# The keys' weights on ScalarE in place of GpSimd, and the bonus selector in one instruction

## The chip, the cores and the metric

The kernel runs on one core of a Trainium2 chip. The metric is the device time in microseconds (us) of one execution. An execution has five engines that work side by side, each strictly in the order of its own queue: TensorE (PE: matmuls; its weight loads are PEld), VectorE (DVE), ScalarE (ACT), GpSimd (POOL) and SyncE (SP), which here issues the loads of the weights.

## The reference, cut to what matters

Two layers over 256 tokens of width 1024, in float32. Layer 0 is an RWKV-7 time mix and a SwiGLU feed-forward block, layer 1 a rotary block attention and another feed-forward block. The change is in the time mix of layer 0:

```python
xr, xw, xk, xv, xa, xg = [x + xx * mu[n] for n in range(6)]
r, k, v = jnp.einsum('nbtc,ncd->nbtd', jnp.stack([xr, xk, xv]), w_rkv)
a = jax.nn.sigmoid(a0 + (xa @ a1) @ a2)
g = jax.nn.sigmoid(xg @ g1) @ g2
kk = heads(k * k_k)
kk = kk / jnp.maximum(jnp.sqrt(jnp.sum(kk * kk, -1, keepdims=True)), 1e-12)
k = k * (1 + (a - 1) * k_a)          # the keys' weights
...                                  # decays, the recurrence over time: y
bonus = jnp.sum(rh * kh * r_k, -1, keepdims=True) * vh
y = (y + bonus.reshape(B, T, C)).astype(x.dtype)
return (y * g) @ w_o
```

The weight of a key is a * k_a + (1 - k_a): one multiplication and one addition, with k_a and 1 - k_a constant along the tokens. The sum in the bonus is a matmul with a selector of heads that carries r_k.

## The kernel before

Channels lie on the 128 partitions, tokens along the free dimension, so a vector over channels is a column of `vec`, and an operation on 128 channels and 256 tokens is a 128x256 instruction.

**Weights.** Each weight matrix arrives in pieces of 512 KB over SP's queue into three raw buffers (`Stream.run`). ACT casts a piece to `hi`, a rounded copy, and DVE (or POOL for pieces listed in `PL`) computes `lo = raw - hi`. PE multiplies hi and lo separately, so a product of 128x512 is three matmuls. A raw buffer is free again when `lo` is done.

**Order of work.** The kernel is a set of generators (`weigh`, `keys`, `inverse`, `merge`, `recurrence`, the dense products `v_part` and so on) that yield what they wait for. A planner (`Issue.run`) holds a cost model of the engines (`Clock`), asks each generator when it could go on, and takes the ready one of the lowest rank. What it issues becomes each engine's fixed order. So a change of one instruction's engine or cost also changes the order in which later instructions stand on every engine. `yield I.idle("DVE")` makes a part wait until the modelled DVE is free. A generator added with the flag `True` (thin) is passed over where the model sees TensorE's clock low.

**The time mix.** `decays`, `gate` and `norms` give E (the decays), a and the raw kk (`kkr`) on ACT; `weigh(u)`, for u = 0 to 3, makes the weights `ka` of two slices of 128 channels in one half-slot and multiplies k by them on DVE, then makes `KB` and `a<-a,E`, which read the exponentials E. `on("ka")` is POOL since "ka" stands in the list `OFF`. `start()` makes `selrk`, the selector of the bonus. Later `scores` give the matrices SC of each chunk of 64 tokens, and `inverse` inverts their 32x32 diagonal blocks by 31 steps of two DVE operations on `TT`; DVE then transposes the result into `TN` and back into `SC` (STREAM_TRANSPOSE), and `merge` joins the blocks on PE: the products `n` (from TN) and then `t` (from SC and TN). After t the recurrence over the chunks (z, u, s, y) begins. The matmuls `v` (256 tokens by 1024 values) and `g` have no part in that chain; PE does them where the planner sees it free. Every engine instruction is recorded at the helper's line L300, so groups below go by tiles:

```python
yield ev(f"TN{hp}")
for q, hs in parts:
    for i in range(16):
        mm(nps[q][hi, i * 32:(i + 1) * 32], blk(hp, 0, 1)[:, q * 16 + i, :], TN[lo, q * 16 + i, :], True, True)
    I.after(nps[q][hi], lambda q, hs: act.copy(out=TN[hi, hs, :], ...), q, hs)
yield from fill(FILLI[hp])
yield ev(f"back1{hp}")
```

In this `merge`, `fill` lets a few v matmuls in before t.

Of the kernel before, what the change touches and what calls it, by code (L numbers as in the profile page):

```python
# [10 lines left out]
AF = mybir.ActivationFunctionType  # L11
ALU = mybir.AluOpType
# [7 lines left out]
KT = D // 128  # L20
# [39 lines left out]
NARROW = (slice(0, 512), slice(512, 768), slice(768, 1024))  # L60
LAST = ((WIDE, WIDE), (WIDE, NARROW))
OUTS = (1, 1)
OFF = ('ka', 'kk1', 'xxv')
MIXR = 'dve'
MIXA = "dve"
BON = 'pool'
# [28 lines left out]
MU, W0, A0, KK, KA, RK, GNG, GNB = 0, 48, 56, 64, 72, 80, 88, 96  # L95
# [327 lines left out]
def trunk(ctx, tc, a, out):  # L423
    nc = tc.nc
    clk = Clock()
    act, dve, pool = Engine(tc, nc.scalar, "ACT", clk), Engine(tc, nc.vector, "DVE", clk), Engine(tc, nc.gpsimd, "POOL", clk)
# [20 lines left out]
    def slot(shape, name, dtype=F32):  # L447
        return tp.tile([128] + shape, dtype, tag="t4", name=nm(name))
# [4 lines left out]
    def half_slot(name, dtype=F32):  # L453
        return sm.tile([128, 2, T], dtype, tag="w2", name=nm(name), bufs=6)

    I = Issue(clk)
    E = {}

    def ev(name):
        return E.setdefault(name, Event())  # L460
# [9 lines left out]
    def mm(ps, lhsT, rhs, start, stop, **kw):  # L470
        pe.matmul(ps, lhsT, rhs, start=start, stop=stop, **kw)
# [15 lines left out]
    vec = const.tile([128, 104], F32, name="vec")  # L487
# [5 lines left out]
    for u in range(4):  # L493
        q, o = u // 2, (u % 2) * 2
# [10 lines left out]
    sel2 = cst[:, 512:514]  # L505
# [3 lines left out]
    omka = const.tile([128, 8], F32, name="omka")  # L509
    dve.tensor_scalar(omka, vec[:, KA:KA + 8], -1.0, 1.0, ALU.mult, ALU.add)  # L510
    selrk = const.tile([128, KT, 2], F32, name="selrk")
# [28 lines left out]
    def c4(x):  # L540
        return x.rearrange("p a (c t) -> p a c t", c=NC)

    def on(name):
        return pool if name in OFF else dve

# [95 lines left out]
    def shifts():  # L641
        for u in range(4):
            q, o = u // 2, (u % 2) * 2
            yield xT[q][:, o:o + 2, :]
            pool.tensor_tensor(xx[q][:, o:o + 2, :], xT[q][:, o:o + 2, 0:T], xT[q][:, o:o + 2, 1:T + 1], ALU.subtract)
# [46 lines left out]
    av, Ev = [slot([4, T], "a") for _ in range(2)], [slot([4, T], "E") for _ in range(2)]  # L692
# [80 lines left out]
    def norms(u):  # L773
# [5 lines left out]
        sq = half_slot("sq")  # L779
        if "sq" in OFF:  # L780
            pool.tensor_tensor(sq, kkr[g][:, o:o + 2, :], kkr[g][:, o:o + 2, :], ALU.mult)
# [31 lines left out]
    def weigh(u):  # L813

        g, o = u // 2, (u % 2) * 2
        yield ev(f"k{u}")
        yield ev(f"a{g}")
        yield I.idle("DVE")
        w = half_slot("ka")
        for j in range(2):  # L820
            p = u * 2 + j
            on("ka").tensor_scalar(w[:, j, :], av[g][:, o + j, :], vec[:, KA + p:KA + p + 1], omka[:, p:p + 1],
                              ALU.mult, ALU.add)
        for j, x in enumerate(ksrc[u]):
            js = slice(0, 2) if len(ksrc[u]) == 1 else j
            dve.tensor_tensor(kg[g][:, o:o + 2, :][:, js], x, w[:, js], ALU.mult)
        I.reach(ev(f"ka{u}"), kg[g][:, o:o + 2, :])
        yield ev(f"G{g}")
        yield I.idle("DVE")
        for hp in range(2):  # L830
            r = HALF[hp]
            on(f"kb{hp}").tensor_tensor(KB[u][r, :, :, hp, :], c4(kg[g][r, o:o + 2, :]), c4(Gi[g][r, o:o + 2, :]), ALU.mult)
        yield I.idle("DVE")
        on("av").tensor_tensor(av[g][:, o:o + 2, :], av[g][:, o:o + 2, :], Gi[g][:, o:o + 2, :], ALU.mult)
        I.reach(ev(f"kd{u}"), KB[u], av[g][:, o:o + 2, :])
# [825 lines left out]
    def start():  # L1661
        mix(0, "xk", 2, early_slot, True)
        yield from shifts()
        I.reach(ev("xx"), *xx)
        mix(2, "xr", 0, early_slot, eng=dict(pool=pool, dve=dve)[MIXR])
        yield ev("xr")
        for p in range(KT):
            pool.tensor_scalar(selrk[:, p, :], sel2, vec[:, RK + p:RK + p + 1], None, ALU.mult)

    I.add(0, start())  # L1670
    I.add(0, W.run())
    I.add(1, lora())
    for g in range(2):
        I.add(1, decays(g))
    for u in range(4):
        I.add(2, norms(u), True)
        I.add(3, weigh(u))
# [97 lines left out]
```

## Time and profile before

| what | value |
|---|---|
| median of three runs | 750.04 us (747.36 to 753.28) |
| the profiled execution: time, span | 746.08 us, 744.3 us |
| mean granted clock of TensorE in it | 0.959 of full |
| busy: PE / PEld / DVE / ACT / POOL | 689.4 / 587.6 / 539.7 / 382.2 / 185.0 us |
| share of the span | 93% / 79% / 73% / 51% / 25% |

The busy shares are means over a program with stages of different limits, and idle time of an engine that nobody waits for costs nothing. A matmul's record ends late by its pipeline, so the pace of a row of matmuls is read from start to start. The granted clock stands in tenths or as a fraction of full speed: 1.00 is 2.4 GHz and 0.50 is 1.2 GHz.

### The profile page before, as it was taken

What the parts mean: (1) busy time and instruction counts of PE and PEld (TensorE: products, weight loads), DVE (VectorE), ACT (ScalarE), POOL (GpSimd) and SP (SyncE); (2) the same over time, 40 slices, a digit from 0 to 9 for tenths busy, and PEclk for the clock granted to TensorE, in tenths of its full rate; (3) what the DMA queues carried; (4) which work ended last, traced back from release to release, by engine and by line L of the source; (5) the groups of instructions that cost most, each with busy time, mean ns of one, the idle gap of its engine ahead of it and who ended that gap; (6) DMA issues with size and microseconds to landing.
All of it is one profiled execution on the core that took longest, in us unless ns stands there. A gap on an engine that the chain in (4) does not pass through costs nothing.

```text
span 744.3 us, 11759 instructions
## 1 busy us (share of the span) xinstructions
PE 689.4 (93%) x4500; PEld 587.6 (79%) x4500; DVE 539.7 (73%) x915; ACT 382.2 (51%) x679; POOL 185.0 (25%) x132
## 2 busy tenths in 40 slices
PE   6899795998889999999999699999979999999995
PEld 5799684777678888888888488777769888888885
DVE  7989999948897766656657935977776665666576
ACT  5974134456545554554556324756635545545550
POOL 5777964343463000000001613113040000000000
PEclk9999898779899999999999889999989999999999
DMA  6445312120565655655557615345046556555551
GB/s 242 152 147 187 107 57 86 57 83 7 188 223 172 227 178 190 196 183 187 197 182 240 201 34 182 125 142 199 28 170 195 178 194 197 175 194 192 187 160 56
DMA packets 33576, 117.21 MB, mean 157 GB/s; under 512 B 3808, under 2 KB 4832, under 8 KB 33520
## 3 DMA queue, kind: packets, MB, share of 16 engines
q1 hardware_dynamic: 31936, 110.89, 44.6%
q10 hardware_dynamic: 1584, 5.57, 2.5%
q8 instruction: 35, 0.57, 0.3%
q14 instruction: 21, 0.17, 0.1%
HBM read 115.40 MB, written 1.05 MB: 156 GB/s over the span
## 4 chain that ended last, share of the span: by engine, by line
PE 68%; DVE 8%; ACT 2%; DMA 2%; issue 1%; DVEq 0%; ACTq 0%
PE gu L300 29%; PE acc L300 14%; PE qkv L300 9%; PE o L300 5%; DVE xtok L300 3%; PE gn L300 2%; PE v L300 1%; PE tr L300 1%; DMA raw<-in_w_qkv_dram 1%; DVE sc L300 1%; PE ptr L300 1%; PE pv L300 1%; PE n L300 1%; ACT hi L300 1%; PE att L300 1%
## 5 line engine op out<-in xcount | busy, mean ns | idle before, releaser
L300 DVE TENSOR_TENSOR lo<-raw,hi 128x1024 fp32r<-128x1024 f32 (+1 forms) x172 | 210.3, 1228 | 144.6 <-ACT hi L300 144.4
L300 ACT CAST hi<-raw 128x1024 fp32r<-128x1024 f32 (+1 forms) x214 | 212.0, 999 | 186.2 <-issue 93.1
L300 PE MATMUL gu<-xw,hi 128*128 128x512 f32 x640 | 226.1, 395 | 0.0
L300 PE MATMUL gu<-xw,lo 128*128 128x256 f32 x640 | 179.8, 281 | 0.0
L300 POOL TENSOR_TENSOR lo<-raw,hi 128x1024 fp32r<-128x1024 f32 (+1 forms) x41 | 87.8, 2158 | 261.3 <-ACT hi L300 257.6
L300 PEld LDWEIGHTS gu<-xw,hi 128*128 128x128 f32 x640 | 120.3, 188 | 27.1
L300 PEld LDWEIGHTS gu<-xw,lo 128*128 128x128 f32 x640 | 120.9, 189 | 0.7
L300 PE MATMUL acc<-hi,hl 128*128 128x512 f32 (+1 forms) x180 | 53.8, 369 | 0.0
L300 PE MATMUL acc<-lo,hh 128*128 128x512 f32 (+1 forms) x180 | 53.7, 368 | 0.0
L300 PE MATMUL acc<-hi,hh 128*128 128x512 f32 (+1 forms) x180 | 53.5, 366 | 0.0
L300 PE MATMUL qkv<-hi,xhi 128*128 128x512 f32 x96 | 40.7, 424 | 2.3 <-ACT xhi L300 2.3
L300 PE MATMUL qkv<-hi,xlo 128*128 128x512 f32 x96 | 39.3, 409 | 0.0
L300 ACT ACTIVATE silu<-silu 128x256 f32<-128x256 f32 x40 | 16.7, 417 | 44.0 <-DVE silu L300 44.0
L300 PE MATMUL qkv<-lo,xhi 128*128 128x512 f32 x96 | 39.0, 406 | 0.0
L300 PEld LDWEIGHTS acc<-hi,hl 128*128 128x128 f32 x180 | 32.8, 188 | 6.2
L300 PEld LDWEIGHTS acc<-lo,hh 128*128 128x128 f32 x180 | 32.7, 188 | 5.6
L300 PEld LDWEIGHTS acc<-hi,hh 128*128 128x128 f32 x180 | 31.8, 188 | 6.0
L300 PE MATMUL o<-hi,xhi 128*128 128x512 f32 x64 | 28.6, 447 | 3.0 <-ACT xhi L300 3.0
L300 PE MATMUL o<-lo,xhi 128*128 128x512 f32 x64 | 27.5, 430 | 0.0
L300 PE MATMUL o<-hi,xlo 128*128 128x512 f32 x64 | 27.3, 429 | 0.0
L300 POOL TENSOR_TENSOR ro<-ro 128x512 f32<-128x512 f32 x8 | 12.1, 1515 | 57.1 <-DVE ro L300 57.1
L300 PE MATMUL gn<-hi,xw 128*128 128x256 f32 x128 | 24.4, 287 | 0.4 <-ACT xw L300 0.3
(227 smaller groups left out, 1292.5 us busy)
## 6 DMA issues: line engine op xcount, KB each, us to landing
raw<-in_w_in_dram SPq DMA_DIRECT2D x80, 512.0 KB, 3.3
raw<-in_w_dn_dram SPq DMA_DIRECT2D x44, 512.0 KB, 3.3
raw<-in_w_qkv_dram SPq DMA_DIRECT2D x24, 512.0 KB, 3.4
raw<-in_w_o_dram SPq DMA_DIRECT2D x20, 512.0 KB, 3.5
raw<-in_w_r_dram SPq DMA_DIRECT2D x8, 512.0 KB, 3.4
raw<-in_w_v_dram SPq DMA_DIRECT2D x8, 512.0 KB, 3.3
raw<-in_w_if_dram SPq DMA_DIRECT2D x8, 512.0 KB, 3.6
raw<-in_w_k_dram SPq DMA_DIRECT2D x6, 512.0 KB, 3.8
```

The costliest lines, as they stand in the source:

```text
L300: ins = f(*args, **kw).ins
```

## The change

The eight `tensor_scalar` of `weigh` (two for each u, 128x256) leave POOL; ACT computes the same value as an `activation` with the function Identity, scale k_a and bias 1 - k_a. In `weigh` the part now yields for the weights and for DVE behind these two instructions, where it yielded for DVE ahead of them. And `selrk` becomes one POOL `tensor_tensor` over 128x16, where it was eight `tensor_scalar` of 128x2.

```diff
-OFF = ('ka', 'kk1', 'xxv')
+OFF = ('kk1', 'xxv')
...
-        yield I.idle("DVE")
         w = half_slot("ka")
         for j in range(2):
             p = u * 2 + j
-            on("ka").tensor_scalar(w[:, j, :], av[g][:, o + j, :], vec[:, KA + p:KA + p + 1], omka[:, p:p + 1],
-                              ALU.mult, ALU.add)
+            act.activation(w[:, j, :], av[g][:, o + j, :], AF.Identity, scale=vec[:, KA + p:KA + p + 1],
+                           bias=omka[:, p:p + 1])
+        yield w
+        yield I.idle("DVE")
...
-        for p in range(KT):
-            pool.tensor_scalar(selrk[:, p, :], sel2, vec[:, RK + p:RK + p + 1], None, ALU.mult)
+        pool.tensor_tensor(selrk, sel2[:, None, :].to_broadcast([128, KT, 2]),
+                           vec[:, RK:RK + KT, None].to_broadcast([128, KT, 2]), ALU.mult)
```

The planner then orders the program anew. Three places matter below. The first is ACT at the place of the first weights; TABLE_LOAD is the load of a table of functions, kkr a pass over two PSUM results k, and E (with G, its inverse) the exponentials that `KB` and `a<-a,E` need. Before:

```order
L300 ACTIVATE a_110<-z_367,vec 128x256 x2
L300 ACT_TABLE_LOAD
L300 ACTIVATE G_113<-E_111 128x16x64
L300 ACTIVATE kkr_118<-k_345,vec 128x256 x2
L300 ACTIVATE E_111<-E_111 128x1024
L300 ACTIVATE G_114<-E_112 128x16x64
L300 ACTIVATE sq_485<-kkr_118 128x512
L300 ACTIVATE E_112<-E_112 128x1024
L300 CAST hi_501<-raw_384 128x1024
```

And now:

```order
L300 ACTIVATE a_110<-z_360,vec 128x256 x2
L300 ACTIVATE ka_430<-a_109,omka,vec 128x256 x2
L300 ACTIVATE ka_457<-a_109,omka,vec 128x256 x2
L300 ACTIVATE kkr_118<-k_338,vec 128x256 x2
L300 ACT_TABLE_LOAD
L300 ACTIVATE G_113<-E_111 128x16x64
L300 ACTIVATE G_114<-E_112 128x16x64
L300 ACTIVATE E_111<-E_111 128x1024
L300 ACTIVATE E_112<-E_112 128x1024
L300 CAST hi_491<-raw_377 128x1024
```

Four ka stand there now (two rows of two), the kkr stands ahead of the table load, and the two G ahead of the two E. The other four ka stand between casts further on.

The second is DVE in the same place. Before:

```order
L300 TENSOR_TENSOR k_116<-k_116,ka_437 128x512
L300 TENSOR_TENSOR lo_387<-raw_265,hi_386 128x1024
L300 TENSOR_TENSOR k_116<-k_345,ka_475 128x512
L300 TENSOR_TENSOR KB_130<-k_116,E_111 64x8x64 x2
L300 TENSOR_TENSOR a_109<-a_109,E_111 128x512 x2
L300 TENSOR_TENSOR lo_502<-raw_384,hi_501 128x1024
L300 TENSOR_TENSOR KB_131<-k_116,E_111 64x8x64 x2
```

And now:

```order
L300 TENSOR_TENSOR lo_380<-raw_265,hi_379 128x1024
L300 TENSOR_TENSOR k_116<-k_116,ka_430 128x512
L300 TENSOR_TENSOR k_116<-k_338,ka_457 128x512
L300 TENSOR_TENSOR a_109<-a_109,E_111 128x512 x2
L300 TENSOR_TENSOR lo_492<-raw_377,hi_491 128x1024
L300 TENSOR_TENSOR KB_130<-k_116,E_111 64x8x64 x2
L300 TENSOR_TENSOR KB_131<-k_116,E_111 64x8x64 x2
```

The products a<-a,E and the lo of the next piece stand ahead of all four KB, where the first two KB stood first.

The third is PE where `merge` begins, behind the last g. There n takes TN from DVE; rows of n and t are 16 small matmuls each, and the profile records two for each. Before (19 v stand ahead of the first n, the last two of which are shown):

```order
L300 MATMUL v_1437<-hi_1334,xlo_868 128x512
L300 MATMUL v_1437<-hi_1399,xhi_867 128x512
L300 MATMUL n_1425<-TN_167,SC 32x32 x16
L300 MATMUL n_1426<-TN_167,SC 32x32 x16
L300 MATMUL v_1437<-lo_1400,xhi_867 128x512
L300 MATMUL v_1437<-hi_1399,xlo_868 128x512
L300 MATMUL n_1425<-TN_167,SC 32x32 x16
L300 MATMUL v_1437<-hi_1399,xhi_867 128x512
L300 MATMUL n_1426<-TN_167,SC 32x32 x16
L300 MATMUL v_1437<-lo_1400,xhi_867 128x512
L300 MATMUL v_1437<-hi_1399,xlo_868 128x512
L300 MATMUL v_1549<-hi_1289,xhi_865 128x512
```

Eight more v stand between these rows and the first t. And now, from the last two g on:

```order
L300 MATMUL g_1386<-hg_151,hi_1208 128x256
L300 MATMUL g_1386<-hg_151,hi_1247 128x256
L300 MATMUL n_1412<-TN_167,SC 32x32 x16
L300 MATMUL n_1413<-TN_167,SC 32x32 x16
L300 MATMUL v_1501<-hi_1282,xhi_858 128x512
L300 MATMUL v_1501<-lo_1283,xhi_858 128x512
L300 MATMUL n_1412<-TN_167,SC 32x32 x16
L300 MATMUL n_1413<-TN_167,SC 32x32 x16
L300 MATMUL v_1501<-hi_1282,xlo_859 128x512
L300 MATMUL v_1501<-hi_1282,xhi_858 128x512
L300 MATMUL v_1501<-lo_1283,xhi_858 128x512
L300 MATMUL v_1501<-hi_1282,xlo_859 128x512
```

The 19 v that stood ahead of the first n stand behind the last n now, so that 31 v come between the last n and the first t, where it was 11. From the end of `merge` on, PE's order is nearly that of before, and SP's order is the same throughout.

## Rows read from the trace of the kernel before

**Rows 1.** The page's chain that ended last, by engine.

```profile
PE 68%; DVE 8%; ACT 2%; DMA 2%; issue 1%; DVEq 0%; ACTq 0%
```

**Rows 2.** Windows, all engines: busy us (count), granted clock, DMA share, GB/s.

```profile
66.00:142.00 76.00, 62.29 (x423) 55.78 (x421) 74.34 (x159) 28.57 (x47) 46.74 (x28) 0.89 0.25 82
```

**Rows 3.** Timeline of PE from 128 to 164: start, length, what, count [idle before].

```profile
130.23 0.80 PE L300 MATMUL g<-hg,hi 128*128 128x256 f32 x2 [8.03 <-DVE hg L300]
...
136.87 0.40 PE L300 MATMUL v<-hi,xhi 128*128 128x512 f32 x1
...
139.66 0.39 PE L300 MATMUL v<-hi,xhi 128*128 128x512 f32 x1
...
142.83 2.21 PE L300 MATMUL n<-TN,SC 32*32 32x32 f32 x64 [0.60 <-DVE TN L300]
...
147.48 1.91 PE L300 MATMUL n<-TN,SC 32*32 32x32 f32 x32
149.32 0.80 PE L300 MATMUL v<-lo,xhi 128*128 128x512 f32 x1
149.91 0.63 PE L300 MATMUL v<-hi,xlo 128*128 128x512 f32 x1
...
152.90 0.63 PE L300 MATMUL v<-hi,xhi 128*128 128x512 f32 x1
...
154.00 1.20 PE L300 MATMUL t<-SC,TN 32*32 32x32 f32 x32
```

**Rows 4.** Timeline of DVE in the same stretch.

```profile
140.74 3.96 DVE L300 STREAM_TRANSPOSE TN<-TT 32x1024 f32<-32x1024 f32 x2
144.73 7.93 DVE L300 STREAM_TRANSPOSE SC<-TT 32x1024 f32<-32x1024 f32 x4
```

**Rows 5.** Windows of PE: busy us (count), granted clock, DMA share, GB/s.

```profile
123.00:130.00 7.00, 0.00 (x0) 0.73 0.16 62
130.00:136.00 6.00, 5.77 (x25) 0.50 0.00 0
136.00:142.00 6.00, 5.47 (x26) 0.96 0.09 18
...
147.00:153.50 6.50, 6.50 (x43) 0.50 0.00 0
```

**Rows 6.** Timeline of POOL from 14 to 66.

```profile
15.18 7.11 POOL L300 TENSOR_SCALAR selrk<-cst,vec 128x2 f32<-128x2 f32 x8 [2.03 <-DMA cst<-in_consts_dram]
...
22.82 2.34 POOL L300 TENSOR_TENSOR lo<-raw,hi 128x1024 fp32r<-128x1024 f32 x1
...
32.34 5.31 POOL L300 TENSOR_SCALAR ka<-a,vec,omka 128x256 f32<-128x256 f32 x4
```

**Rows 7.** Timeline of DVE from 15 to 70.

```profile
22.34 3.37 DVE L300 TENSOR_TENSOR xlo<-mx,xhi 128x512 fp32r<-128x512 f32 x1
...
26.20 0.69 DVE L300 TENSOR_TENSOR xlo<-mx,xhi 128x512 fp32r<-128x512 f32 x1
...
38.53 0.69 DVE L300 TENSOR_TENSOR k<-k,ka 128x512 f32<-128x512 f32 x1 [1.30 <-ACT kkr L300]
39.41 1.38 DVE L300 TENSOR_TENSOR KB<-k,E 64x512 f32<-64x512 f32 x2 [0.18 <-ACT E L300]
40.80 1.30 DVE L300 TENSOR_TENSOR a<-a,E 128x512 f32<-128x512 f32 x2
42.76 1.30 DVE L300 TENSOR_TENSOR lo<-raw,hi 128x1024 fp32r<-128x1024 f32 x1 [0.66 <-ACT hi L300]
...
50.92 5.43 DVE L300 TENSOR_TENSOR lo<-raw,hi 128x1024 fp32r<-128x1024 f32 x3
```

**Rows 8.** Timeline of ACT from 28 to 56.

```profile
35.34 1.28 ACT L300 ACT_TABLE_LOAD   x1
...
37.61 0.82 ACT L300 ACTIVATE kkr<-k,vec 128x256 f32<-128x256 f32 x2
38.31 1.06 ACT L300 ACTIVATE E<-E 128x1024 f32<-128x1024 f32 x1
```

## The prediction

> **What bounds the kernel now.** I read the page first, its chain that ended last: the matmuls carry 68% of the span [rows 1]. A change that touches no matmul therefore matters only where PE waits for the engines it does touch. I looked for that place next in the timeline of PE. From 123 to 130 PE does nothing [rows 5], since it waits 8.03 us for DVE's hg, and from 142.83 n begins on DVE's TN [rows 3]. The window 66 to 142 says why PE waits there: DVE is busy 74.34 of 76.00 us, PE 62.29, ACT 28.57 [rows 2]. So DVE's queue sets when TN comes, and a microsecond that DVE wins or loses ahead of 66 reaches TN, less what the idle 1.66 us of this window swallow. Between g and n, before, PE has 19 matmuls v to do, from 136.87, and then waits only 0.60 us for TN. From n to t PE never waits [rows 3]: it is PE that sets when t starts, 154.00, and t begins the chain of the recurrence. DVE's transposes back into SC, which t needs too, end at 152.66 (144.73 + 7.93) [rows 4], 1.3 us ahead of it.
>
> **The selector.** Eight instructions, 7.11 us from 15.18, become one. The mean of the eight is 0.89 us, and one with sixteen elements in place of two should cost about that, so POOL is free 6 us earlier. What gains is only what stood behind: POOL's lo at 22.82, which lay beside DVE's xlo. That xlo took 3.37 us where its like took 0.69 [rows 6, 7]. At worst the lo waits for its hi and nothing comes of it, at best the whole stretch of 2.7 us goes. I take 0.4 us, since POOL's lo was due to begin half a microsecond after the xlo and still has its 2.34 us of work to do beside DVE's.
>
> The Trainium skill gives a reason for that stretch ("SBUF — State Buffer", section "Who interferes with whom"): a DVE instruction with two SBUF inputs contends with a GpSimd instruction that reads SBUF, and one of them holds the shared pair of ports for its whole length. The 3.37 against 0.69 us of xlo agrees. By this rule taking eight reading instructions from GpSimd speaks for a gain on DVE, and it is the ground of the first rival.
>
> **The weights on ACT.** No row shows this activation. The nearest is kkr, also 128x256 with a scale from `vec`: two in 0.82 us [rows 8], 0.41 each. I take 0.43, with 0.35 and 0.6 as bounds; eight make 3.4 us (2.8 to 4.8). The first four, 1.7 us, stand where the table load stood, at 35.34, and end at 37.1; behind them kkr starts at 37.61 as before, since it waits for k from PE, so the four ka are hidden in that wait, also at 0.55 each. The price is what they displace: the table load (1.28 us) began at 35.34 and must now wait behind kkr, which ends at 38.43. So: load to 39.7, two G (as long as E, 1.06 us) to 41.7, the first E to 42.7. Before, that E began at 38.31 and ended at 39.4 [rows 8]: 3.3 us later.
>
> Who waits for that is DVE. After its second k (until 39.2) it stands at a<-a,E, with lo and all KB queued behind, until 42.7, so 3.5 us; two a take 1.3 us; the hi behind the two E comes at 44.7, another 0.6. With the 1.30 ahead of k, which stay, that is 5.4 us of idle time in place of 1.30 + 0.18 + 0.66 = 2.14 [rows 7], a loss of 3.3. Against it stands what ka held up on DVE. From the rows this is little: the product a<-a,E at 40.80 took 1.30 us for two though ka lay beside it, and only the first of the three lo at 50.92 (5.43 us against 1.30 each, 1.5 too much) met the last ka until 51.3; half of the 1.5, 0.8 us, goes [rows 6, 7]. The other four ka stand among casts where ACT has idle time and cost the path nothing; with that cover gone they would cost 1.7.
>
> At 66 DVE is then late by -0.4 + 3.3 - 0.8 = +2.1 us, of which the 1.66 idle us up to 142 [rows 2] swallow none to all; I take half. So TN comes **1.3 us** later, at 144.1. Bounds: -1.0 (the whole 2.7 at the selector, all of the slack) and +3.3 (no gain at the selector or from ka, no slack).
>
> A rule of the skill speaks against this place of the weights ("ScalarE: Activation LUTs", section "Rules for kernel authors"): add and mul belong on VectorE, not ScalarE. Here DVE's 74.34 of 76.00 us speak against following it: on DVE the same 3.4 us would all go onto TN, and the forecast would be some 2 us later than it is, not earlier.
>
> **The order of PE.** This is the largest term. The 19 v that filled PE while DVE finished TN now stand behind n. PE is through with g at 136.87 and then waits for TN until 144.1, 7.2 us without a matmul (5.9 if g, which waits for DVE's hg, shifts with DVE). PE's work does not shrink, so the 19 v, 0.2325 us each (136.87 to 139.66 in 12 steps), 4.4 us, are now done behind n. In addition the clock falls: after the 7.00 idle us of 123 to 130 the granted clock was 0.50 from 130 to 136, and again 0.50 from 147 to 153.5 [rows 5]. After the new wait I expect the lower level, too. At 0.50 thirty-two n take 1.84 us (147.48 to 149.32), so the 128 take 7.4 us, where at full clock 64 took 2.14, 4.3 in all. A v takes 0.427 at this level (149.91 to 152.90 in 7 steps).
>
> How long it stays there I take from two places: g began at 130.23 and the clock rose near 136.5, 6.3 us; the v from 149.32 were at the upper level from about 153.4, 4.1 us [rows 3, 5]. From 144.1: n 7.4, two v 0.85, then 31 v, of which 4.1 us (9.6 v) or 6.3 us (14.8 v) at the lower level and the others at 0.2325: 9.1 or 10.1 us. So t starts at 161.5 or 162.5 in place of 154.00, **7.5 to 8.5 us** later. DVE's SC, at 154.0, has long been there. Everything from t to the end hangs on t, PE's order is nearly the same there, and I see nothing that takes the delay up. Sum: 746.08 + 8.0 = 754.1 against the profiled execution; this one lies 3.96 us under the median of the three runs (750.04), so **758** as a median.
>
> **Rivals.** First, the way to the other side: PE's wait for TN doesn't come, since TN comes before g is done. The mechanism is the lock between POOL and DVE: xlo's 2.7 us and the 1.5 of the three lo are 4.2 us of stretch in the rows that POOL's shrinking could take away, more in rows like them. It decides from 5.8 us on (142.83 less 137.0). Then n starts at 137.0 at full clock, 4.3, with 33 v at 0.2325, 7.7: t at 149.0, 5.0 us earlier, so 745. Against it: the later E, 3.3 us, and what POOL still has to do, which stays. Chance 0.08.
>
> Second, PE waits but the clock doesn't fall, or rises as n begins: from 144.1, 4.3 + 7.7 give t at 156.1, +2.1 us, 752. For it: in the rows the n from 142.83 ran at full clock after a wait of 0.60. Against it: the wait is some ten times as long. Chance 0.15.
>
> Third, the clock stays at the lower level through the v as well: 7.4 + 33 x 0.427 = 21.5, t at 165.6, +11.6 us, 762; with TN at its late bound 764. For it: in the old order the clock fell while n ran, without a long wait. Against it: in the v from 149.32 it came back after 4.1 us. Chance 0.17.
>
> Fourth, the new order is there but something later swallows it, so that nothing measurable remains: 750 to 751. PE's waits behind t would have to be for work that doesn't hang on t; I found none. Chance 0.08.
>
> **How the numbers follow.** The forecast has 0.52, the rivals 0.08, 0.15, 0.17 and 0.08. One per cent, 7.5 us, is about what a measurement of this kernel can tell from no change. The forecast at 8.0 lies on this bound; with TN between -1.0 and +3.3 it goes from 755 to 760, and I put 0.30 of its 0.52 above 757.5, so slower is 0.30 + 0.17 = 0.47, and faster (under 742.5) only the far end of the first rival, 0.05; the rest, 0.48, is the same. The range, 750 to 763, leaves out the first rival and the ends of the third.
>
> **What would show it.** In the profile after: selrk one instruction; ACT's first E ending near 42.7 and DVE waiting for it 3.5 us; g, then a wait of PE for DVE's TN near 7 us, n at a granted clock of 0.50, and 31 v between the last n and t. PE's later order would be shifted as a whole. The forecast is wrong if TN comes before 140, if n runs at full clock, or if t starts before 159.

## The result, and the profile after

The changed kernel took 758.17 us (median of four runs, 755.20 to 761.59), the kernel before 748.81 us on the same chip; the ratio is 1.0127 with a 95% interval of 1.0082 to 1.0171, so it is slower, by less than 2%. The profiled execution took 755.20 us against 746.08, 9.1 us more, and its span is 753.2 us. The median forecast was 758. **The number held, although the delay behind it was mis-sized by several microseconds, as the rows show.**

The chain that ended last, which answers to [rows 1], now has DVE in it with 26%, where it had 8%:

```profile
PE 64%; DVE 26%; ACT 4%; issue 3%; DMA 2%; DVEq 0%; ACTq 0%; SPq 0%
```

The timeline of ACT, which answers to [rows 8]:

```profile
35.66 2.21 ACT L300 ACTIVATE ka<-a,omka,vec 128x256 f32<-128x256 f32 x4
37.63 0.96 ACT L300 ACTIVATE kkr<-k,vec 128x256 f32<-128x256 f32 x2
38.61 1.28 ACT L300 ACT_TABLE_LOAD   x1
39.91 2.02 ACT L300 ACTIVATE G<-E 128x1024 f32<-128x1024 f32 x2
41.83 1.99 ACT L300 ACTIVATE E<-E 128x1024 f32<-128x1024 f32 x2
43.72 1.03 ACT L300 CAST hi<-raw 128x1024 fp32r<-128x1024 f32 x1
```

As forecast, the four ka end about when kkr can start (37.63, before 37.61), the table load stands behind kkr, and the first E ends near 42.8. From the first ka to kkr it is 1.97 us, 0.49 for each of the four, where 0.43 was assumed. By the Trainium skill ("ScalarE: Activation LUTs", section "What ACT_TABLE_LOAD costs": 186 ns, 0.833 ns an element, 93 ns for each pointer operand, 93 ns of overlap) an estimate is 0.49; the trace agrees.

DVE in the same place, which answers to [rows 7]; the bracket is the idle time before, and what ended it:

```profile
35.22 1.23 DVE L300 TENSOR_TENSOR lo<-raw,hi 128x1024 fp32r<-128x1024 f32 x1 [0.63 <-ACT hi L300]
36.92 0.69 DVE L300 TENSOR_TENSOR k<-k,ka 128x512 f32<-128x512 f32 x1 [0.48 <-ACT ka L300]
38.63 0.69 DVE L300 TENSOR_TENSOR k<-k,ka 128x512 f32<-128x512 f32 x1 [1.01 <-ACT kkr L300]
42.90 1.29 DVE L300 TENSOR_TENSOR a<-a,E 128x512 f32<-128x512 f32 x2 [3.58 <-ACT E L300]
44.78 1.23 DVE L300 TENSOR_TENSOR lo<-raw,hi 128x1024 fp32r<-128x1024 f32 x1 [0.59 <-ACT hi L300]
...
70.65 1.23 DVE L300 TENSOR_TENSOR lo<-raw,hi 128x1024 fp32r<-128x1024 f32 x1 [0.86 <-ACT hi L300]
71.79 0.68 DVE L300 TENSOR_TENSOR kkr<-kkr,rb 128x512 f32<-128x512 f32 x1
```

The waits named in the forecast are there: 3.58 for E, 0.59 for the hi behind it. But so are others: 0.63 and 0.48 ahead of the first k, 0.86 for a hi just ahead of `kkr<-rb`. This kkr starts at 71.79, before at 66.28: 5.5 us later, where 2.1 was forecast. The windows of all engines (PE, PEld, DVE, ACT, POOL busy) up to about that instruction, and DVE alone from the second k (38.53, now 38.63) to it, first before, then after:

```profile
28.00:66.00 38.00, 36.70 (x303) 36.15 (x303) 35.64 (x38) 27.42 (x45) 29.26 (x20) 0.96 0.49 159
...
38.53:66.28 27.75, 26.69 (x26) 1.00 0.52 169
```

```profile
28.00:72.00 44.00, 37.47 (x296) 36.20 (x295) 36.67 (x38) 31.65 (x54) 18.27 (x12) 0.95 0.43 139
...
38.63:71.79 33.16, 28.00 (x26) 0.95 0.41 132
```

Of 38.00 us DVE idled 2.36 before; of 44.00 it idled 7.33 now. Its work up to kkr came to about 35.9 us then (38.28 less 2.36) and 36.5 now (43.79 less 7.3), although POOL was busy 18.27 us in place of 29.26. So the locks that the ka caused were worth nothing to DVE on balance: ahead of the second k its work is 0.8 us less, and that k is only 0.1 us late; behind it the work is 1.3 us more. There the same products meet POOL's lo and mx, for example (two KB took 1.38 us at 39.41 before):

```profile
52.34 2.98 DVE L300 TENSOR_TENSOR KB<-k,E 64x512 f32<-64x512 f32 x2
```

```profile
51.28 3.48 POOL L300 TENSOR_TENSOR mx<-xx,vec 128x512 f32<-128x512 f32 x2
```

The selector brought DVE nothing. POOL's lo, which stood behind it, still waited for its hi and began at 22.84, before at 22.82. The stretch went from xlo (0.69 us now) to the lr behind it (2.45 us, before 0.42).

The end of the inverse, on DVE, and POOL's lo beside it:

```profile
143.39 2.45 DVE L300 TENSOR_TENSOR tmp<-LT,TT 128x16 f32<-128x16 f32 x2
145.76 2.41 DVE L300 TENSOR_TENSOR TT<-TT,tmp 128x16 f32<-128x16 f32 x2
148.26 3.82 DVE L300 STREAM_TRANSPOSE TN<-TT 32x1024 f32<-32x1024 f32 x2
```

```profile
143.45 4.68 POOL L300 TENSOR_TENSOR lo<-raw,hi 128x1024 fp32r<-128x1024 f32 x2 [17.03 <-ACT hi L300]
```

Before, only one pair of these last steps was long:

```profile
138.19 2.46 DVE L300 TENSOR_TENSOR TT<-TT,tmp 128x16 f32<-128x16 f32 x2
```

TN begins at 148.26, 7.5 us later than in [rows 4]. Of the 5.5 at kkr nothing had been swallowed up to g (135.65 against 130.23, 5.4); the rest is the second long pair of steps, 2.1 us. PE, which answers to [rows 3], and its windows, to [rows 5]:

```profile
141.97 0.40 PE L300 MATMUL g<-hg,hi 128*128 128x256 f32 x2
150.23 3.62 PE L300 MATMUL n<-TN,SC 32*32 32x32 f32 x64 [7.86 <-DVE TN L300]
...
154.93 3.62 PE L300 MATMUL n<-TN,SC 32*32 32x32 f32 x64
158.48 0.80 PE L300 MATMUL v<-hi,xlo 128*128 128x512 f32 x1
...
167.57 2.21 PE L300 MATMUL t<-SC,TN 32*32 32x32 f32 x64
```

```profile
150.00:154.00 4.00, 3.77 (x65) 0.50 0.18 67
...
158.00:162.00 4.00, 4.00 (x19) 0.50 0.00 0
162.00:167.00 5.00, 5.00 (x22) 0.97 0.00 0
```

This part went as forecast: PE waits 7.86 us, n runs at a granted clock of 0.50, 7.4 us of n in 2 x 3.62, the clock is back near 162, and the 31 v take 9.1 us (158.48 to 167.57). From n to t it is 17.3 us; 17.4 to 18.4 were forecast, and 11.2 stood there before. So t starts at 167.57, **13.6 us later**, not 7.5 to 8.5. And yet the end is only 8.9 us later. By z (174.32, before 161.57) 12.75 us are left: from t to z the granted clock was 0.92 before and 1.00 now, and the three v just ahead of z took 1.40 us then and 0.89 now. At the first gu of the feed-forward block it is 11.7. From there to the first qkv of the second layer it took 178.2 us before and 176.7 now, so 1.5 more go.

How much of this belongs to the change, another trace tells: the run with the weights alone (below) has the same order of PE. There t starts at 166.95, 12.95 us later than before, z at 173.71, and the span is 755.6 us, 11.3 us longer. Only 1.6 us are taken up. From z to the end it took 581.9 us, before 582.7, in the changed kernel 578.9, the least of all fourteen traces. From gu to qkv, 8 of the 12 other traces lie between 176.3 and 177.1, kernels with the weights on POOL among them. So by these traces most of the 4.7 us that are taken up between t and the end (13.6 less 8.9) lies in the two executions and not in the change.

### The profile page after: what moved, and what is told of

Read it like the earlier page. It is cut to its first block, busy times and chain, and to the rows that moved or that the text cites. A ratio compares the mean times of both kernels' runs of the same rounds, so it can differ in the third digit from the quotient of the medians.

```text
span 753.2 us, 11749 instructions
## 1 busy us (share of the span) xinstructions
PE 685.6 (91%) x4500; PEld 585.3 (78%) x4500; DVE 539.8 (72%) x915; ACT 385.7 (51%) x687; POOL 167.2 (22%) x117
## 4 chain that ended last, share of the span: by engine, by line
PE 64%; DVE 26%; ACT 4%; issue 3%; DMA 2%; DVEq 0%; ACTq 0%; SPq 0%
PE gu L300 28%; PE acc L300 13%; PE qkv L300 9%; DVE xtok L300 5%; DVE lo L300 3%; DVE tmp L300 2%; DVE TT L300 2%; PE v L300 2%; PE o L300 2%; PE gn L300 2%; DMA raw<-in_w_dn_dram 1%; PE tr L300 1%; DVE mx L300 1%; DVE KB L300 1%; ACT hi L300 1%
## 5 line engine op out<-in xcount | busy, mean ns | idle before, releaser
L300 POOL TENSOR_TENSOR ro<-ro 128x512 f32<-128x512 f32 x8 | 12.1, 1516 | 56.5 <-DVE ro L300 36.5
```

Source lines behind the costliest of these rows:

```text
L300: ins = f(*args, **kw).ins
```

## The experiments

Ratios are to runs of the kernel before beside them on the same chip; microseconds are worked out from the ratios. One microsecond is 0.13%.

**The two edits apart.** Selector alone (the `start()` hunk of the diff on the kernel before), and weights alone (the other hunks).

> The kernel before with the selector in one instruction and nothing else; the order of every engine is that of before but for POOL's seven missing instructions. Theory (the selector's time was hidden but for 0.4 us of DVE stretch): within 1 us of before, 748 to 750. Rival (the earlier POOL moves its lo into other DVE work and costs): 2 us or more above before.

> The changed kernel with the eight selector instructions of before. Theory (all of the loss comes with the weights on ACT and the order that follows from them): as the changed kernel, 757 to 759, TN near 150. Rival (the selector's earlier end on POOL has a share): 2 us or more away from the changed kernel.

The selector alone: 750.95 us in ten runs, ratio 1.0037 (1.0002 to 1.0072), 2.8 us. That is the size of this run's rival and not of its theory, though the interval goes nearly down to no change. The weights alone: 757.76, 1.0157 (1.0121 to 1.0193). So the loss comes with the weights; whether the selector adds a little is open, since the two edits together gave 1.0127, no more than the weights alone. The profiled execution of the selector alone was the slowest of its ten (756.1), with the order of before on DVE and ACT. Its kkr came 0.4 us and its g 0.6 us later than before, but then the end of the inverse on DVE, the lo on POOL beside it, and n on PE read:

```profile
138.11 2.53 DVE L300 TENSOR_TENSOR tmp<-LT,TT 128x32 f32<-128x32 f32 x2
140.56 2.46 DVE L300 TENSOR_TENSOR TT<-TT,tmp 128x32 f32<-128x32 f32 x2
...
143.89 3.82 DVE L300 STREAM_TRANSPOSE TN<-TT 32x1024 f32<-32x1024 f32 x2
```

```profile
138.19 4.79 POOL L300 TENSOR_TENSOR lo<-raw,hi 128x1024 fp32r<-128x1024 f32 x2 [16.60 <-ACT hi L300]
```

```profile
145.86 3.43 PE L300 MATMUL n<-TN,SC 32*32 32x32 f32 x64 [3.55 <-DVE TN L300]
```

Here two pairs of steps met POOL's lo. TN came 3.15 us later than before, some 2.5 of it behind g, and PE waited 3.55 us in place of 0.60. From n to t the granted clock was 0.51 where it had been 0.69, from t to z 0.68 where it had been 0.92, and PE waited for nothing there. So the 3.0 us at n became 5.8 at t and 7.8 at z (169.37). Whether this is what spreads the runs of the kernel before from 743 to 756 us is asked below.

**PE's order, both ways.** First the changed kernel with v held ahead of n, then the kernel before with v held behind n. The event `vm` is reached when the last of the v that are to stand ahead has been issued, or the last n, and `ahead[0]` is that instruction:

```diff
+        yield ev("vm")
         yield ev(f"TN{hp}")
         for q, hs in parts:
+            pe.held = ahead[0]
```

```diff
+        yield ev("vm")
         for hf in range(2):
...
+                    pe.held = ahead[0]
                     v_part(ps, ws[q], hf, q, (kk,))
```

> The changed kernel with the 19 v held ahead of the first n again. Theory A (two losses, a TN that is some 7 us late and the v behind n): PE waits about 2.5 us for a TN near 150, t starts near 161.5 in place of 167.6, and the time is 751 to 753. Theory B (the order of PE is nearly all of the loss): as before, 748 to 750. Theory C (the late TN is nearly all of it and the order costs nothing): as the changed kernel, 757 to 759.

> The kernel before with all v of the second half held behind the n of merge, TN as early as before (142.8). Theory A (the order alone, at an early TN): a PE wait near 6 us, n at a granted clock of 0.50, t at 160 to 162, and 755 to 758. Theory C (the order costs nothing): as before, 748 to 750. A clock that stays at full speed would give about 750.

> The kernel before with the same rule as in the changed kernel with v first (19 v held ahead of n), a control for what this rule does to the order behind z. Theory (that order costs what the changed kernel with v first won at z, 5.8 us between z and the first gn): z as early as before, gn 4 to 7 us later, 752 to 755. Rival (the loss behind z comes from the late TN): 747 to 749.

> The changed kernel with 12 v held ahead of n; the order that follows has 19 v there, as before, and behind z it keeps the places of the changed kernel more nearly than the run with 21 v. Theory A (late TN and PE's order are two separate losses): TN near 149 as in the changed kernel, t 5 to 7 us earlier than there, and 751 to 755. Theory C (with a late TN the order is worth nothing): as the changed kernel and as the run with 21 v, 757 to 760.

The kernel before with v behind n: 753.38, 1.0080 (1.0047 to 1.0113), 6.0 us, which lies between the two theories (755 to 758, and 748 to 750). Its PE rows, in an execution in which TN itself was late by 4.4 us:

```profile
147.10 6.84 PE L300 MATMUL n<-TN,SC 32*32 32x32 f32 x128 [8.43 <-DVE TN L300]
...
163.73 2.21 PE L300 MATMUL t<-SC,TN 32*32 32x32 f32 x64
```

From n to t 16.6 us pass, where it was 11.2. So the order costs 5.5 us at t with no edit of the weights.

The changed kernel with v ahead came out at 759.03, 1.0181 (1.0139 to 1.0223), as theory C had it. But its rows say otherwise at t: 160.72 in place of 167.57, and z 6.5 us earlier. The gain went behind z, where holding v (21 of them in place of 19) had changed other places too. The control shows that: the kernel before with the same rule took 751.36, 1.0054 (1.0020 to 1.0088). Its z came 1.3 us later than before, but its first gu 6.2 us later; its PE waits behind z include these, which were 0.3 and nothing before:

```profile
PE u L300 <- ACT zs L300: 2.1, 4, 1.0
PE gn L300 <- POOL lo L300: 2.0, 2, 1.1
```

Against this control, with PE's order nearly equal, the late DVE can be read by itself. The changed kernel with v ahead has kkr<-rb 4.7 us later (71.19 against 66.52), t 5.4 (160.72 against 155.36) and the end 5.4 (754.5 against 749.1): the delay goes through whole.

With 12 v held, 19 stand ahead of n as before and the order behind z changes less: 755.94, 1.0085 (1.0043 to 1.0127), between its two theories. In its profile (759.0, among its slower ones) n and t read:

```profile
151.10 3.07 PE L300 MATMUL n<-TN,SC 32*32 32x32 f32 x64 [3.33 <-DVE TN L300]
...
164.65 2.58 PE L300 MATMUL t<-SC,TN 32*32 32x32 f32 x64
```

13.6 us from n to t in place of 17.3, with TN as late as in the changed kernel. So the order is worth 3.8 us at t. In the time it is 3 to 5 us (1.0085 against 1.0127 and 1.0157), but the intervals overlap. That is less than at an early TN: PE still waits 3.3 us for TN with nothing left to do, and from 154 to 162 n and v run at 0.50 all the same.

**The late E without the weights.** The kernel before, weights on POOL, with table load and exponentials held behind the second pair of kkr (`kk1[0]`):

```diff
         yield Ev[g]
+        yield ev("kk1")
+        act.held = kk1[0]
         act.activation(G[g][:, :, :, 1:C + 1], c4(Ev[g]), AF.Exp, scale=-DEC)
```

> The kernel before (weights on POOL) with the table load and the exponentials held behind the second pair of kkr on ACT, as they stand in the changed kernel; PE's order is that of before, with the 19 v ahead of n. Theory (the late E is what makes TN late): E ends near 42.7, DVE waits for it some 3 us and kkr<-rb, 66.3 before, begins 3 to 5 us later; TN comes 3 to 5 us later, PE waits for it 3 us or more and the clock falls with it; 752 to 756. Rival (DVE fills the wait and the lateness comes from the weights themselves): 748 to 750 with kkr<-rb within 1 us of before.

753.01 us, 1.0057 (1.0015 to 1.0100), 4.3 us. On DVE, and then PE's n:

```profile
42.58 1.61 DVE L300 TENSOR_TENSOR KB<-k,E 64x512 f32<-64x512 f32 x2 [3.17 <-ACT E L300]
...
57.15 1.23 DVE L300 TENSOR_TENSOR lo<-raw,hi 128x1024 fp32r<-128x1024 f32 x1 [2.87 <-ACT hi L300]
...
69.54 0.68 DVE L300 TENSOR_TENSOR kkr<-kkr,rb 128x512 f32<-128x512 f32 x1
```

```profile
146.20 2.21 PE L300 MATMUL n<-TN,SC 32*32 32x32 f32 x64 [0.60 <-DVE TN L300]
```

The wait for E is 3.17 us, near the 3.58 of the changed kernel. It brings a second: DVE's lo are late, so PE's last k is late; on ACT a kkr that waits 7.17 us for this k stands in front of the next hi, and DVE waits 2.87 us for that hi. kkr<-rb begins at 69.54, 3.3 us late; in the changed kernel it is 5.5. So E's place makes a delay of the larger part of that size, and not of all of it. The 3.3 us then go through unchanged: 3.4 at t (157.35) and at z (164.93), 3.7 at the end (748.0). The longer wait of PE and the lower clock that the theory expected did not come, since g waits for DVE as well and comes 3.4 us later with TN: PE waits 0.60 us, as before.

**The weights on ACT behind the exponentials, and on DVE** (there `'ka'` is taken from `OFF`, and the selector is one instruction). Both with v held (21 ahead of n), so that the control above and the changed kernel with v ahead are their measure:

```diff
         yield ev(f"a{g}")
+        yield ev(f"G{g}")
         w = half_slot("ka")
```

> The changed kernel with the weights behind the exponentials on ACT (E where it stood before) and 19 v held ahead of n; to be read against the control with v forced and against the changed kernel with v first. Theory (the late E and what hangs on it is the whole delay of TN): kkr<-rb within 1.5 us of the control's 66.5 and the time within 2 us of the control, 750 to 754. Rival (the weights on ACT delay the keys and the casts wherever they stand): kkr<-rb at 68.5 or later and 755 or more.

> Selector in one instruction, and the weights on DVE, by the Trainium skill's rule, with 19 v held ahead of n. E stands on ACT where it stood before. Theory (DVE has no room): eight weights of 0.25 to 0.45 us add 2 to 3.5 us to DVE's queue less at most 2 us of waits that they fill; TN 1 to 3 us later than in the control with v forced, and 1 to 5 us above that control. Rival (the rule holds here: DVE's gain of free ports and filled waits is larger): at or below the control.

Behind the exponentials: 761.28, 1.0168 (1.0092 to 1.0244). The first E ends at 39.2, as before, and it doesn't help:

```profile
42.63 1.23 DVE L300 TENSOR_TENSOR lo<-raw,hi 128x1024 fp32r<-128x1024 f32 x1 [6.91 <-ACT hi L300]
...
73.67 0.68 DVE L300 TENSOR_TENSOR kkr<-kkr,rb 128x512 f32<-128x512 f32 x1
```

Now DVE has no k to make, since ka comes behind E, and waits 6.91 us at another place. Its kkr is later still, 73.67. My theory for this run fell: not E's place alone costs. As I read it, one engine has ka and E to do in the same 10 us, and DVE waits for the one or the other. But kkr's 7.4 us are not what reaches PE: in this order two KB and an AR stand ahead of kkr that stood behind it, and TN comes at 144.17, 3.4 us later than before. PE doesn't wait for it. DVE's hg stands later among the steps of the inverse, so g is late (138.69), most of the 21 v come behind g, and n begins at 151.69. So this run shows that time is lost with ka behind E too, and not that it is lost at TN. On DVE: 753.52, 1.0076 (1.0037 to 1.0115). The ka there:

```profile
L300 DVE TENSOR_SCALAR ka<-a,vec,omka x8: 385/404/2478, 34.3 to 62.2; 128x256 f32<-128x256 f32 x8
```

The median is 0.40 us (one took 2.48), kkr<-rb begins at 70.15, 3.9 us later than before. And yet TN is not late:

```profile
141.07 4.20 DVE L300 STREAM_TRANSPOSE TN<-TT 32x1024 f32<-32x1024 f32 x2
```

That is 0.3 us later than before and 1.1 earlier than in the control (142.18). Again two KB stand ahead of kkr that stood behind it, g is late (135.64), and n begins at 149.02 without a wait for TN. With the same rule for v the engines thus stand: weights on POOL 1.0054, on DVE 1.0076, on ACT 1.0181 or 1.0168. POOL and DVE are not told apart, since their intervals overlap and the run on DVE has the selector in one instruction; the weights on ACT ahead of the exponentials are slower than both, behind them slower than on POOL. The change also moved the yield for DVE in `weigh` behind the weights, and that place was not tested by itself.

**POOL's lo beside the inverse.** First its last two pieces on DVE (`'v': [2, 3, 4, 5]` in `PL`), then on POOL but behind a copy of a column of TT, so that they begin when the inverse has ended (the two pieces are held by `W.hold`, not shown), with 15 and with 12 v ahead of n:

```diff
+        pool.tensor_copy(out=done_tt, in_=TT[:, 0, 31:32])
+        pool.held = pool.last
```

> The kernel before with the lo of the last two v pieces on DVE in place of POOL, so that POOL reads nothing beside the last steps of the inverse; PE has 24 v ahead of n by the order that follows. Theory (the lo of POOL stretches the last TT or tmp steps by 2.2 us each, once or twice): no step of 2.4 us is left there, TN within 1 us of before (two lo more on DVE, 2.3 us, against 2.2 to 4.4 of stretch) and less scatter between executions: 745 to 749. Rival (DVE pays the two lo in full): 2 to 5 us above before.

> The kernel before with the last two lo of v on POOL made to wait for the end of the inverse (a copy of one column of TT ahead of them), and 12 v held ahead of n. Theory (the lo of POOL beside the last steps of the inverse costs TN 2.2 us, in some executions 4.4, and with a longer wait the clock): no step over 0.6 us there, TN begins 2 us earlier from the same start of the inverse, and 742 to 747. Rival (the lo, later by as much, make PE wait between n and t or ahead of n): 748 to 753.

> As the run with the last two lo of v behind the inverse, but with exactly 12 v ahead of the first n, so that no v that needs a late lo stands ahead of n (there PE waited 2.01 us for that lo and n ran at the lower clock). Theory (the gain at TN was lost to that wait and its clock): n begins near 139.5, 1.5 us earlier than in that run, after a wait of some 1 us; at full clock t comes near 149.5 and the time is 742 to 746; if the clock falls all the same, t near 153 to 154 and 746 to 749. Rival (something other than n bounds t, DVE's SC or the lo): t no earlier than 155, 749 to 752.

On DVE: 752.11, 1.0041 (1.0005 to 1.0077): DVE pays them in full, since it also waits 1.65 us for their hi. Behind the inverse with 15 v: 749.54, 1.0004 (0.9974 to 1.0034). TN begins 3.3 us earlier, but one v ahead of n now waits for its lo, and the n behind it run at 0.50 from the first:

```profile
137.47 3.93 DVE L300 STREAM_TRANSPOSE TN<-TT 32x1024 f32<-32x1024 f32 x2
```

```profile
139.91 0.80 PE L300 MATMUL v<-lo,xhi 128*128 128x512 f32 x1 [2.01 <-POOL lo L300]
...
141.06 3.62 PE L300 MATMUL n<-TN,SC 32*32 32x32 f32 x64
```

The ten runs lie between 748.2 and 751.8, the 19 runs of before beside them between 745.2 and 755.9. With exactly 12 v ahead:

```profile
139.20 2.21 PE L300 MATMUL n<-TN,SC 32*32 32x32 f32 x64 [0.84 <-DVE TN L300]
...
142.47 3.62 PE L300 MATMUL n<-TN,SC 32*32 32x32 f32 x64
...
151.61 1.19 PE L300 MATMUL t<-SC,TN 32*32 32x32 f32 x32
```

PE waits 0.84 us, the first 64 n run at full clock and the others at half, t starts at 151.61, 2.4 us earlier than before and between the two forecasts of its theory, and the time is 747.40 against 750.68, ratio 0.9967 (0.9932 to 1.0001). This is the only version whose ratio is below 1, by 0.3%, and its interval just reaches 1. The scatter, however, is back: its twelve runs lie between 745.1 and 754.8, those of before beside them between 746.1 and 756.4, though the two lo stand behind the inverse here too; and with the lo on DVE it was 744.8 to 753.9. So POOL's lo beside the inverse is not shown to be what spreads the runs, and the narrow ten runs may come from n being at half clock from the first.

## Why the prediction came out, step by step

**What bounds, right.** PE's wait for TN is the place, DVE's queue sets it, and E's later end is DVE's longest wait: forecast 42.7 and 3.5 us, measured 42.90 (a's start) and 3.58.

**The delay of TN, mis-sized: forecast 1.3 us (bounds -1.0 to +3.3), measured 7.5.** At kkr 2.1 us were forecast, as -0.4 + 3.3 - 0.8, and 5.5 measured, and each of the three terms was off. The selector's 0.4 us did not come: it was the case that the forecast named as the worst, POOL's lo waiting for its hi. The idle time of DVE grew by 5.0 us, not 3.3. 0.9 of that lies ahead of the second k (for a hi and for ka itself) and was paid back by 0.8 less work there; 4.1 lies behind it, the wait for E and 0.86 for a late hi. And in place of the 0.8 us taken off for ka's locks, DVE worked 1.3 us more behind that k, beside POOL's other work. After kkr the 1.66 us of slack swallowed nothing (DVE idles 3.60 us there now, and works as long as before), while a second pair of the last steps met POOL's lo, 2.1 us. The rows showed that this could happen: one such pair of 2.46 us stood there before. The lower bound doesn't follow from its terms either: -2.7 + 3.3 - 0.8 is -0.2, and slack can swallow a delay but not make a lead.

**The order of PE, right in kind and size.** n at 0.50, 31 v in 9.1 us, 17.3 us from n to t. Undone and done by itself it is worth 3 to 6 us. That PE's wait was 7.86 us where 7.2 was forecast is luck: the 7.2 had g in its old place, and g came 5.4 us later along with DVE; with g shifted, the forecast's own number was 5.9.

**"I see nothing that takes the delay up", mostly right, as far as the traces tell.** 4.7 of the 13.6 us at t are gone at the end between the two profiled executions, but only 1.6 of 12.95 in the run with the weights alone, and nothing where PE's order is equal (5.4 us at t, 5.4 at the end). What took up the rest in the one execution is not settled.

So the number held by luck in its terms: t was forecast 8.0 us late and came 13.6. Part of the difference is the execution that the forecast started from: at 746.08 us it was among the fast ones of before (median 748.81), so a typical execution may have had less to lose, which no trace here shows. An estimate from the weights-only run: 11.3 us between the profiles, less the 1.9 us that 746.08 lies under the median of before beside it (747.94), gives 9.4; 9.8 was measured there, and 9.4 for the change. The 8.0 us were thus 1.4 too few, and the median of before came out 1.2 lower than the 750.04 to which they were added. The two prices, each measured with the other absent, 4.3 us for the late E and 6.0 for the order, add up to 10.3; the measured difference lies within their intervals, which are wide.

**The rivals.** TN early enough to do without the wait: no sign of it, DVE's work up to kkr did not shrink (36.5 us, before 35.9). A clock that stays up: no, 0.50 through all of n. A clock that stays down through v: no, back near 162. Something later that swallows the delay: no, 9.4 us are left. **The rule weighed against the trace.** The Trainium skill ("ScalarE: Activation LUTs", section "Rules for kernel authors") puts add and mul on VectorE, not ScalarE. The forecast set this aside since DVE was busy, and the times of the runs side with the rule: 1.0076 (1.0037 to 1.0115) on DVE, 1.0181 (1.0139 to 1.0223) on ACT, each with v held. The forecast had all of DVE's 3.4 us reach TN; kkr did come 3.9 us later, but TN only 0.3, in another order of the planner. And ACT's price was 5.5 us at kkr where 2.1 was counted.

## What to carry to other kernels

An engine with idle time on average may have none in the 10 us in which the work would be put: look at the queue there, and at what stands behind the moved instructions in it. Where PE waits for a chain, count not only the wait but the clock behind it, and look for the filler that the new order has moved to the wrong side of the wait. A sum that comes out right is no proof of its terms: compare each with its row.

## What the runs showed of the hardware that was not expected

Steps of 128x16 on DVE, some 0.3 us for a pair, took 2.4 us when they met a lo of POOL of 2.4 us. They wait, then, about as long as the whole POOL instruction lasts, however small they are. The Trainium skill ("SBUF — State Buffer", section "Who interferes with whom") calls the pair of ports that the two engines share an exclusive lock, and the trace agrees. The transposes TN behind them were hardly touched by such a lo: 3.96 us for two beside one before, 3.82 without one now. And such a slip can decide more than its own length: 3.0 us at n became 7.8 at z in one execution, with n and v at the lower clock. A delay that shifts g along with TN, and so leaves PE's wait at 0.60 us, was not multiplied in that way: 3.3 us at kkr, 3.7 at the end.
